# Sparse attention: masks and positions added by VectorE together with the row maximum

## The chip, the cores and the metric

The program runs on one core of one Trainium2 chip. A core has five engines with queues of their own: TensorE (PE; its weight loads are shown apart as PEld), VectorE (DVE), ScalarE (ACT), GpSimd (POOL) and SyncE (SP, which here only issues transfers). The metric is the time of one execution on the device in microseconds (us); lower is better. The kernel before was timed in three runs, and one more execution was profiled.

## The reference, cut to what matters

The model is a decoder trunk of two layers over 512 tokens with width 1024. Layer 1 has, between two feed-forward halves, an attention with three branches over 16 heads of 64, in two groups of keys and values. The change lies in two of the branches, `selected` and `sliding`. With 512 tokens the selection takes all blocks and the window holds all earlier tokens, so both are plain causal softmax attention with positions by slope:

```python
s_s = jnp.einsum('bqghd,bgqnld->bghqnl', qblk, k_sel) - slopes[...] * dist_s
s_s = jnp.where(dist_s >= 0, s_s, NEG)                 # NEG = -1e30
p_s = jax.nn.softmax(s_s.reshape(sh[:4] + (-1,)), axis=-1).reshape(sh)
...
return gblk[..., 0:1] * o_c + gblk[..., 1:2] * o_s + gblk[..., 2:3] * o_w
```

A score is thus q·k, less the head's slope times the distance of query and key, and masked where the key is later than the query. Then `o @ w_out` projects the heads' outputs.

## The kernel before, in words

**Precision.** Products are made of fp32r operands (one pass of TensorE). A value is split into a high part, which fp32r holds exactly, and a low part (the rest). A product then is high x high + high x low + low x high, three matmuls that add up in one PSUM bank (`mm3`, L343 to L345). ScalarE makes the high parts, VectorE or GpSimd the low ones.

**Stages.** `stages` runs `f0, m0, f1, f2, m1, f3, fin`. The change is in `m1` (`mixer1`). Its first part projects keys and values for the two branches (`keys`, `values`), the hidden layer of the compressed branch (`hidden`), and the first queries. Its second part is a loop over steps `t`, written out by hand, whose order of calls is the order of each engine's queue. Its third part is the rest of the output projection.

**Units and steps.** A unit is one pair of heads `m` (8 of them), one head of the two (`hh`) and one branch (`br`): 32 units, three steps each, 96 steps. `m` takes 12 steps. In step t = 3u + x of unit u:

- `scores(u, x)` on TensorE makes the scores of query blocks `JX[x]`: x = 0 blocks 0 and 1 (128 and 256 keys, done with 256 columns each), x = 1 block 2 (384 keys), x = 2 block 3 (512 keys), into one PSUM bank `S` (3 buffers).
- one step later `rowmax` on VectorE takes the negated row maximum, and `exps` on ScalarE writes the exponentials to `P` in SBUF and sums them.
- after the unit's last exponentials `weigh` divides by the sum and applies the branch's gate (VectorE two small instructions, GpSimd four on `P`).
- six steps later `transposes` (TensorE, into one of two PSUM buffers `T`), then `his` (ScalarE) and `lows` (VectorE), which split the transposed weights into `PTh` and `PTl`, and eight steps later `pv` (TensorE) multiplies them with the values into `O`.

Between these the loop puts the query projection of the next m (`qproj`, 24 matmuls of 512 columns, spread over groups of steps by `QP`), its evacuation and split (`qevac` by `QEV`), and the compressed branch of this m (`cmp_step`). From step 77 on no query projection is left; there the table `FILL` puts the split of finished heads' outputs (`osplit`) and the first pieces of the output projection (`oproj`: for output tile d and input tile k, three matmuls of 512 columns).

**The score product before.** `qA` (128 rows) holds q's high part in one half of the partitions and its low part in the other; `kA` holds the keys' high part twice. So one matmul of 128 contraction rows gives high x high + low x high. The second matmul has 68 rows: 64 of q's high part (copied into `qB` by ScalarE or GpSimd) against the keys' low part (`kB`), and four rows that carry the positions (minus slope times query position, in two parts, against ones; the slope in two parts against the key position). Between the two a bf16 matmul adds the mask: the identity (`identb`) times a tile of zeros and -1e30 (`negb`), on the diagonal block. The four rows come by DMA from GpSimd's queue (L1212, L1232).

**What is touched.** `scores`, `rowmax`, `exps` (L1469 to L1505), `qload` and `qevac` (L1224 to L1265), `keys` (L1342), the tiles at the head of `mixer1`, `cmp_step` (a sign), `QEV`, `FILL`, and the constants that `layout` prepares on the host.

Of the kernel before, what the change touches and what calls it, by code (L numbers as in the profile page):

```python
# [20 lines left out]
PLAIN = 2  # L21
DORD = (0, 4, 1, 5, 2, 6, 3, 7)
# [75 lines left out]
def _build(ctx, tc, nc, a, stages):  # L98
# [1096 lines left out]
    def mixer1(nm, nxt):  # L1195
        with ExitStack() as c:
# [3 lines left out]
            identb = sb.tile([128, 128], BF, name="identb")  # L1200
            V.tensor_copy(identb, ident)
            negb = sb.tile([128, 128], BF, name="negb")
# [5 lines left out]
            for br in range(2):  # L1208
                for g in range(2):
                    kA[br, g] = sb.tile([128, T], F32R, name=f"kA{br}{g}")  # L1210
                    kB[br, g] = sb.tile([68, T], F32R, name=f"kB{br}{g}")
                    P.dma_start(kB[br, g][64:68, :], a["keyrows"])  # L1212
                    VS[br, g], V3[br, g] = VSa[:, 2 * br + g], V3a[:, 2 * br + g]
# [11 lines left out]
            def qload(m):  # L1225
                t = aq.tile([128, 4, 2, 32], F32, name="cb", bufs=2)
                nc.sync.dma_start(t, a["cbias"][m])
                bias[m] = t
                qb = []
                for hh in range(2):  # L1230
                    b_ = aq.tile([128, T], F32R, name="qB", bufs=4)
                    P.dma_start(b_[64:68, :], a["qrows"][2 * m + hh])  # L1232
                    qb.append(b_)
                qst[m] = [None, None, qb]
# [10 lines left out]
            def qevac(m, step):  # L1245


                if step == 0:
                    qf = aq.tile([128, T], F32, name="qf", bufs=2)
                    V.scalar_tensor_tensor(qf, qp.pop(m)[0], 0.125, nm.rstd, op0=OP.mult, op1=OP.mult)  # L1250
                    qst[m][0], qst[m][1] = qf, []
                    return
                hh, step = divmod(step - 1, 3)
                r, r2 = slice(hh * 64, hh * 64 + 64), slice(64 - hh * 64, 128 - hh * 64)
                if step == 0:
                    qst[m][1].append(aq.tile([128, T], F32R, name="qA", bufs=3))
                    S.activation(qst[m][1][hh][r, :], qst[m][0][r, :], AF.Copy)
                    return
                t = qst[m][1][hh]
                if step == 1:  # L1260
                    V.tensor_sub(t[r2, :], qst[m][0][r, :], f32(t[r, :]))
                elif hh:
                    P.tensor_copy(qst[m][2][hh][0:64, :], f32(t[r, :]))
                else:
                    S.activation(qst[m][2][hh][0:64, :], f32(t[r, :]), AF.Copy)  # L1265
# [26 lines left out]
            with ExitStack() as c2:  # L1292
                s2 = c2.enter_context(pool("m1t", 1, reuse_waits="tile"))
                ps = c2.enter_context(pool("m1p", 2, space=PSUM, reuse_waits="tile"))
                neg = s2.tile([128, 128], F32, name="neg")
                nc.sync.dma_start(neg, a["neg"])
# [40 lines left out]
                V.tensor_copy(negb, neg)  # L1337
# [4 lines left out]
                def keys(br, key):  # L1342
                    p = pj()
                    proj(p, W.next(key), nm)
                    W.pump(3)
                    kf = s2.tile([128, T], F32, name="kf", bufs=2)
                    V.tensor_mul(kf, p, rstd)
                    k2 = s2.tile([64, T], F32, name="k2", bufs=2)
                    V.tensor_mul(k2, p[64:128, :], rstd[64:128, :])
                    for g in range(2):  # L1350
                        src = kf[0:64, :] if g == 0 else k2
                        S.activation(kA[br, g][0:64, :], src, AF.Copy)
                        S.activation(kA[br, g][64:128, :], src, AF.Copy)
                        V.tensor_sub(kB[br, g][0:64, :], src, f32(kA[br, g][0:64, :]))
# [43 lines left out]
                for part in range(3):  # L1398
# [10 lines left out]
                    if part == 0:  # L1409
                        hidden(1, "v", 2)  # L1410
                        for e in range(4, 7):
                            qevac(0, e)
# [56 lines left out]
            def scores(u, x):  # L1469
                m, hh, br = u  # L1470
                g = m // 4
                qa, qb = qst[m][1][hh], qst[m][2][hh]
                bk = ps.tile([128, T], F32, name="S", bufs=3)
                def half(w, keys, start, stop):
                    for j in JX[x]:
# [3 lines left out]
                                  start=start and j != 1, stop=stop, skip_group_check=True)  # L1479
                        Sb[u, j] = bk[:, c0:c0 + (j + 1) * 128]  # L1480

                half(qa, kA[br, g], True, False)

                if x == 0:
                    d_ = bk.rearrange("p (a b) -> p a b", b=128)[:, 0:4:3, :]
                    TE.matmul(d_, identb, negb[:, None, :].to_broadcast([128, 2, 128]), start=False, stop=False,
                              skip_group_check=True)
                else:
                    j = JX[x][0]
                    TE.matmul(bk[:, j * 128:(j + 1) * 128], identb, negb, start=False, stop=False,  # L1490
                              skip_group_check=True)
                half(qb[0:68, :], kB[br, g], False, True)

            def rowmax(u, x):
                if x == 0:
                    St[u] = at_.tile([128, 64], F32, name="st", bufs=3)[:, 0:16]
                    Pt[u] = at_.tile([128, 1280], F32, name="P", bufs=3)
                for j in JX[x]:
                    V.tensor_reduce(St[u][:, j:j + 1], Sb[u, j], axis=AX.X, op=OP.max, negate=True)

            def exps(u, x):
                st = St[u]
                for j in JX[x]:
                    S.activation(Pt[u][:, OFF[j]:OFF[j] + 128 * (j + 1)], Sb.pop((u, j)), AF.Exp,
                                 bias=st[:, j:j + 1], accum_out=st[:, 4 + j:5 + j])  # L1505
# [59 lines left out]
            def cmp_step(m, step):  # L1565
                if step == 0:
                    p = ps.tile([128, T], F32, name="S", bufs=3)
                    for j in range(4):
# [5 lines left out]
                    V.tensor_add(e, p[:, 0:256].rearrange("p (a b) -> p a b", b=32),  # L1574
                                 bias[m].rearrange("p a h b -> p (a h) b"))
# [42 lines left out]
            QEV = ({8: 0, 9: 1, 10: 2, 12: 3, 14: 4, 16: 6, 19: 5}, {11: 0, 12: 1, 13: 2, 14: 3, 16: 4, 17: 6, 18: 5})  # L1618
# [24 lines left out]
            for m, t in enumerate((78, 79, 81, 83, 86, 90, 97)):  # L1643
                where = (xp, ("xh", 8), ("xl", 8)) if m < 4 else (aq, ("qA", 3), ("qB", 4))
# [153 lines left out]
def layout(i):  # L1798
# [65 lines left out]
    neg = np.where(p[None, :] > p[:, None], f(-1e30), f(0))  # L1864
    slopes = np.array([2.0 ** (-8.0 * (k + 1) / 16) for k in range(16)], dtype=f).reshape(8, 2).T.reshape(16)

    def split(v):
        b = v.astype(f).view(np.uint32)
        hi = (b & np.uint32(0xFFFFF000)).view(f)
        return hi, v.astype(f) - hi  # L1870

    qrows = np.zeros((16, 4, T), f)
    for n in range(16):
        hi, lo = split(-slopes[n] * t.astype(f))
        sh, sl = split(np.full(T, slopes[n], f))
        qrows[n] = np.stack([hi, lo, sh, sl])
    keyrows = np.stack([np.ones(T), np.ones(T), t, t]).astype(f)
    cend = np.arange(31) * 16 + 31
    cb = np.full((8, 128, 4, 2, 32), -1e30, f)
    for m in range(8):  # L1880
# [7 lines left out]
        "poolw": A("a_pool_w")[0].transpose(1, 0, 2).reshape(128, -1), "neg": neg,  # L1888
        "qrows": qrows, "keyrows": keyrows, "cbias": cb,
# [20 lines left out]
```

## Time and profile before

| what | value |
|---|---|
| median of 3 runs | 1874.49 us (1874.49 to 1875.04) |
| profiled execution, its own time | 1873.18 us |
| its span, first to last instruction | 1871.4 us |
| TensorE, matmuls | 1848.3 us, 99% |
| TensorE, weight loads | 1644.1 us, 88% |
| VectorE | 1473.0 us, 79% |
| ScalarE | 968.3 us, 52% |
| GpSimd | 635.7 us, 34% |
| steps 0 to 95 | 1271.9 to 1461.9 us of the span |

A busy time is the union of an engine's instructions, so an engine at 99% has hardly a gap, though a gap-free TensorE may still be slower than it could be: matmuls overlap in its pipeline, and the printed duration of one is longer than the distance to the next start. In the printed forms, `68*128 68x512` is a matmul whose weights have 68 contraction rows and 128 columns, and whose moving operand has 68 rows and 512 columns. fp32r and fp32 both print as f32 there. L1478 is the line of both score products, told apart by `kA` and `kB`.

### The profile page before, as it was taken

How to read it: one execution, taken by the hardware profiler on the slowest of the kernel's cores; microseconds unless marked ns; L12 is line 12 of the kernel's file. 1: busy time of each engine (PE TensorE's matmuls, PEld its weight loads, DVE VectorE, ACT ScalarE, POOL GpSimd, SP SyncE). 2: the span in 40 equal slices, each digit the busy share in tenths (PEclk: the TensorE clock that was granted, in tenths of full speed). 3: DMA queues.
4: the chain of work that ended last, by engine and by line, in shares of the span. 5: the costliest groups of instructions: out<-in, count | busy, mean ns of one | idle time of the engine just before them, and what ended most of it. 6: DMA issues, size and time to landing. Idle time of an engine off the chain costs nothing. (4 is left out here: it accounts for less than half of the span.)

```text
span 1871.4 us, 30811 instructions
## 1 busy us (share of the span) xinstructions
PE 1848.3 (99%) x11564; PEld 1644.1 (88%) x11564; DVE 1473.0 (79%) x2414; ACT 968.3 (52%) x1971; POOL 635.7 (34%) x555
## 2 busy tenths in 40 slices
PE   8999999999999999999999999999999999999998
PEld 6999999778789999998899999878887789999997
DVE  8888887667688888877898887757888679888873
ACT  6445444443455444445454444437888555444443
POOL 2333332203123333312333333114556324333321
PEclk9999999999999999999999999999999999999999
DMA  5232322222233322213223232232100132233221
GB/s 197 80 106 98 109 98 93 85 88 68 79 128 109 102 102 102 102 63 107 102 102 115 100 107 89 88 126 70 30 30 27 57 130 85 102 102 102 102 96 63
DMA packets 62007, 175.12 MB, mean 94 GB/s; under 512 B 7520, under 2 KB 9744, under 8 KB 61856
## 3 DMA queue, kind: packets, MB, share of 16 engines
q1 hardware_dynamic: 60544, 171.68, 27.1%
q8 instruction: 91, 1.49, 0.3%
q10 hardware_dynamic: 576, 1.05, 0.2%
q0 software_dynamic: 736, 0.41, 0.1%
q14 instruction: 60, 0.49, 0.1%
HBM read 171.01 MB, written 2.10 MB: 93 GB/s over the span
## 5 line engine op out<-in xcount | busy, mean ns | idle before, releaser
L542 DVE TENSOR_TENSOR wl<-wr,wh 128x512 fp32r<-128x512 f32 (+1 forms) x312 | 282.1, 926 | 6.0 <-ACT wh L539 2.4
L539 ACT ACTIVATE wh<-wr 128x512 fp32r<-128x512 f32 (+1 forms) x312 | 179.5, 603 | 190.0 <-PE pd L344 172.1
L343 PE MATMUL pd<-ahi,wh 128*128 128x512 f32 x680 | 266.3, 392 | 0.0
L344 PE MATMUL pd<-alo,wh 128*128 128x512 f32 x680 | 266.2, 391 | 0.0
L345 PE MATMUL pd<-ahi,wl 128*128 128x512 f32 x680 | 264.5, 389 | 0.0
L678 DVE TENSOR_TENSOR sl<-T,sh 128x512 fp32r<-128x512 f32 x288 | 242.8, 852 | 22.7 <-ACT sh L677 19.6
L677 ACT ACTIVATE sh<-T 128x512 fp32r<-128x512 f32 x288 | 180.5, 627 | 58.0 <-PE z L714 54.3
L658 POOL TENSOR_TENSOR T<-wg,wr 128x512 f32<-128x512 f32 x36 | 49.8, 1383 | 335.3 <-DMA wg<-in_wts_dram 254.5
L714 PE MATMUL xy<-xh,wl 128*128 128x256 f32 x576 | 163.0, 283 | 0.0
L712 PE MATMUL z<-xs,sh 128*128 128x256 f32 x576 | 163.0, 283 | 0.0
L713 PE MATMUL z<-xs,sh 128*128 128x256 f32 x576 | 163.0, 283 | 0.0
L714 PE MATMUL xy<-xh,sl 128*128 128x256 f32 x576 | 163.0, 283 | 0.0
L713 PE MATMUL xy<-xl,sh 128*128 128x256 f32 x576 | 163.0, 283 | 0.0
L714 PE MATMUL z<-xs,sl 128*128 128x256 f32 x576 | 163.0, 283 | 0.0
L712 PE MATMUL xy<-xh,sh 128*128 128x256 f32 x576 | 163.0, 283 | 0.0
L713 PE MATMUL xy<-xl,wh 128*128 128x256 f32 x576 | 163.0, 283 | 0.0
L712 PE MATMUL xy<-xh,wh 128*128 128x256 f32 x576 | 162.6, 282 | 0.0
L770 DVE SCALAR_TENSOR_TENSOR h<-pd,h 128x512 f32<-128x512 f32 (+1 forms) x157 | 107.1, 683 | 59.9 <-PE pd L345 59.5
L345 PEld LDWEIGHTS pd<-ahi,wl 128*128 128x128 f32 x680 | 127.7, 188 | 27.6
L343 PEld LDWEIGHTS pd<-ahi,wh 128*128 128x128 f32 x680 | 128.2, 189 | 23.1
L344 PEld LDWEIGHTS pd<-alo,wh 128*128 128x128 f32 x680 | 128.2, 189 | 21.4
L658 POOL TENSOR_TENSOR T<-wg 128x512 f32<-128x512 f32 x72 | 108.3, 1504 | 50.6 <-DVE sl L678 50.6
(429 smaller groups left out, 5208.1 us busy)
## 6 DMA issues: line engine op xcount, KB each, us to landing
wr<-in_wts_dram SPq DMA_DIRECT2D x119, 512.0 KB, 3.5
wg<-in_wts_dram SPq DMA_DIRECT2D x72, 512.0 KB, 3.5
wr<-in_wts_dram SPq DMA_DIRECT2D x128, 256.0 KB, 3.7
wf<-in_wts_dram SPq DMA_DIRECT2D x36, 512.0 KB, 4.1
wr<-in_wts_dram SPq DMA_DIRECT2D x32, 384.0 KB, 3.6
h<-in_xt_dram SPq DMA_DIRECT2D x8, 256.0 KB, 4.6
cb<-in_cbias_dram SPq DMA_DIRECT2D x8, 128.0 KB, 3.5
out_dram<-ot ACTq DMA_DIRECT2D x4, 256.0 KB, 2.9
```

Of the source, the lines that this page charges most:

```text
L343: TE.matmul(out, wh, xh, start=first, stop=False)
L344: TE.matmul(out, wh, xl, start=False, stop=False)
L345: TE.matmul(out, wl, xh, start=False, stop=last)
L539: S.activation(w.t[0][:, c], b.t[:, c], AF.Copy)
L542: V.tensor_sub(w.t[1][:, c], b.t[:, c], f32(w.t[0][:, c]))
L658: return lambda: P.tensor_tensor(o.t, x(), y(), op=op)
L677: s = act(T, lambda: S.activation(w.t[0], src(), AF.Copy), (dep,), (w, b))
L678: return w, dve(T, lambda: V.tensor_sub(w.t[1], src(), f32(w.t[0])), (s,), (w, b), True)
L712: TE.matmul(out, wh, xh[:, q], start=start, stop=False, skip_group_check=True)
L713: TE.matmul(out, wh, xl[:, q], start=False, stop=False, skip_group_check=True)
L714: TE.matmul(out, wl, xh[:, q], start=False, stop=k == 3, skip_group_check=True)
L770: return lambda: V.scalar_tensor_tensor(h[d][:, c], b.t[:, c], 0.5, h[d][:, c], op0=OP.mult, op1=OP.add)
```

## The change

The positions and the mask leave TensorE. A host constant `dist` (128 x 512) holds the distance of query and key, 1e30 where the key is later; GpSimd loads it once. For each head GpSimd multiplies it by the slope (`far`, two buffers), three steps before the head's first row maximum. `qevac` gives q the opposite sign, so the bank holds -q·k; VectorE's `tensor_tensor_reduce` then adds the slice of `far`, writes the result to `P` and takes its minimum, and ScalarE's exponential works in place on `P` with scale -1. The second score product has 64 contraction rows: the half of `qA` that holds q's high part, against `kB`, which now holds the keys' low part in both halves. `qB`, its copies, the four rows and the mask products are gone. `QEV` has two entries less for each m. In `FILL` the splits of the outputs move from steps 78-97 to 84-97, and the first tile's pieces from 80, 82, 84, 86, 89, 92, 98 to 88, 90, 90, 94, 94, 96, 98; the second tile's stay.

```diff
+            dist = sb.tile([128, T], F32, name="dist")
+            nc.gpsimd.dma_start(dist, a["dist"])
...
-                    kB[br, g] = sb.tile([68, T], F32R, name=f"kB{br}{g}")
-                    P.dma_start(kB[br, g][64:68, :], a["keyrows"])
+                    kB[br, g] = sb.tile([128, T], F32R, name=f"kB{br}{g}")
...
-                qb = []
-                for hh in range(2):
-                    b_ = aq.tile([128, T], F32R, name="qB", bufs=4)
-                    P.dma_start(b_[64:68, :], a["qrows"][2 * m + hh])
-                    qb.append(b_)
-                qst[m] = [None, None, qb]
+                qst[m] = [None, None]
...
-                    V.scalar_tensor_tensor(qf, qp.pop(m)[0], 0.125, nm.rstd, op0=OP.mult, op1=OP.mult)
+                    V.scalar_tensor_tensor(qf, qp.pop(m)[0], -0.125, nm.rstd, op0=OP.mult, op1=OP.mult)
...
-                if step == 1:
-                    V.tensor_sub(t[r2, :], qst[m][0][r, :], f32(t[r, :]))
-                elif hh:
-                    P.tensor_copy(qst[m][2][hh][0:64, :], f32(t[r, :]))
-                else:
-                    S.activation(qst[m][2][hh][0:64, :], f32(t[r, :]), AF.Copy)
+                V.tensor_sub(t[r2, :], qst[m][0][r, :], f32(t[r, :]))
...
-                        V.tensor_sub(kB[br, g][0:64, :], src, f32(kA[br, g][0:64, :]))
+                        for r in (0, 64):
+                            V.tensor_sub(kB[br, g][r:r + 64, :], src, f32(kA[br, g][0:64, :]))
...
-                qa, qb = qst[m][1][hh], qst[m][2][hh]
+                qa, r = qst[m][1][hh], slice(hh * 64, hh * 64 + 64)
                 bk = ps.tile([128, T], F32, name="S", bufs=3)
-                def half(w, keys, start, stop):
+                for w, keys in ((qa, kA[br, g]), (qa[r], kB[br, g][r])):
                     for j in JX[x]:
                         c0 = 256 if j == 1 else 0
                         n = max(256, 128 * (j + 1))
                         TE.matmul(bk[:, c0:c0 + n], w[:, j * 128:(j + 1) * 128], keys[:, 0:n],
-                                  start=start and j != 1, stop=stop, skip_group_check=True)
+                                  start=w is qa and j != 1, stop=w is not qa, skip_group_check=True)
                         Sb[u, j] = bk[:, c0:c0 + (j + 1) * 128]
 
-                half(qa, kA[br, g], True, False)
-
-                if x == 0:
-                    d_ = bk.rearrange("p (a b) -> p a b", b=128)[:, 0:4:3, :]
-                    TE.matmul(d_, identb, negb[:, None, :].to_broadcast([128, 2, 128]), start=False, stop=False,
-                              skip_group_check=True)
-                else:
-                    j = JX[x][0]
-                    TE.matmul(bk[:, j * 128:(j + 1) * 128], identb, negb, start=False, stop=False,
-                              skip_group_check=True)
-                half(qb[0:68, :], kB[br, g], False, True)
+            far = {}
+
+            def distances(n):
+
+                far[n] = at_.tile([128, T], F32, name="far", bufs=2)
+                P.tensor_scalar(far[n], dist, SLOPES[n], 1.0, op0=OP.mult, op1=OP.mult)
...
                 for j in JX[x]:
-                    V.tensor_reduce(St[u][:, j:j + 1], Sb[u, j], axis=AX.X, op=OP.max, negate=True)
+                    n = 128 * (j + 1)
+                    V.tensor_tensor_reduce(Pt[u][:, OFF[j]:OFF[j] + n], Sb.pop((u, j)), far[2 * u[0] + u[1]][:, T - n:T],
+                                           1.0, 3e38, OP.add, OP.min, St[u][:, j:j + 1])
...
-                    S.activation(Pt[u][:, OFF[j]:OFF[j] + 128 * (j + 1)], Sb.pop((u, j)), AF.Exp,
-                                 bias=st[:, j:j + 1], accum_out=st[:, 4 + j:5 + j])
+                    p = Pt[u][:, OFF[j]:OFF[j] + 128 * (j + 1)]
+                    S.activation(p, p, AF.Exp, bias=st[:, j:j + 1], scale=-1.0, accum_out=st[:, 4 + j:5 + j])
...
-            for m, t in enumerate((78, 79, 81, 83, 86, 90, 97)):
-                where = (xp, ("xh", 8), ("xl", 8)) if m < 4 else (aq, ("qA", 3), ("qB", 4))
+            for m, t in enumerate((84, 84, 87, 89, 90, 92, 97)):
+                where = (xp, ("xh", 8), ("xl", 8)) if m < 4 else (aq, ("qA", 3), ("qB", 1) if m == 6 else ("qf", 2))
...
-            for n, t in enumerate((80, 82, 84, 86, 89, 92, 98, 103, 104, 104, 104, 106)):
+            for n, t in enumerate((88, 90, 90, 94, 94, 96, 98, 103, 104, 104, 104, 106)):
...
                     scores(*at_t(t))
+                if t >= -2 and (t + 2) % 6 == 0 and (t + 2) // 6 < 16:
+                    distances((t + 2) // 6)
```

## Rows read from the trace of the kernel before

**Rows 1.** The page's table of engines: busy us (share) xinstructions.
```profile
PE 1848.3 (99%) x11564; PEld 1644.1 (88%) x11564; DVE 1473.0 (79%) x2414; ACT 968.3 (52%) x1971; POOL 635.7 (34%) x555
```

**Rows 2.** Windows: stretch and length, each engine's busy us, granted clock, DMA.
```profile
1272.00:1425.50 153.50, 152.48 (x988) 128.11 (x987) 127.09 (x314) 125.02 (x372) 85.93 (x137) 1.00 0.10 32
1425.50:1446.20 20.70, 18.53 (x121) 14.92 (x120) 15.76 (x38) 17.37 (x51) 14.59 (x21) 1.00 0.09 27
1446.20:1462.00 15.80, 14.65 (x97) 11.69 (x97) 14.05 (x36) 12.85 (x41) 10.26 (x16) 1.00 0.01 2
1343.02:1366.60 23.58, 23.58 (x158) 19.98 (x155) 19.93 (x49) 19.42 (x58) 13.87 (x22) 1.00 0.09 30
1232.00:1272.00 40.00, 40.00 (x213) 30.91 (x211) 21.91 (x41) 13.26 (x26) 2.54 (x4) 1.00 0.47 166
```

**Rows 3.** Timeline of TensorE, a step with 512 keys: start, duration, line, form.
```profile
1340.45 0.40 PE L1478 MATMUL S<-kA,qA 128*128 128x512 f32 x1
1340.70 0.23 PE L1490 MATMUL S<-negb,identb 128*128 128x128 bf16 x1
1340.74 0.48 PE L1478 MATMUL S<-kB,qB 68*128 68x512 f32 x1
1341.05 0.40 PE L1243 MATMUL X<-xh,wh 128*128 128x512 f32 x1
1341.29 0.40 PE L1243 MATMUL X<-xl,wh 128*128 128x512 f32 x1
```

**Rows 4.** Timeline of TensorE around L915, 48 rows; its third left out.
```profile
373.86 0.39 PE L345 MATMUL pj<-xh,wl 128*128 128x512 f32 x1
374.17 0.69 PE L915 MATMUL at<-grT,gw 48*128 48x512 f32 x1
374.71 0.59 PE L915 MATMUL at<-grT,gw 48*128 48x512 f32 x1
...
375.56 0.59 PE L915 MATMUL at<-grT,gw 48*128 48x512 f32 x1
376.08 0.50 PE L343 MATMUL pj<-xh,wh 128*128 128x512 f32 x1
376.42 0.40 PE L344 MATMUL pj<-xl,wh 128*128 128x512 f32 x1
```

**Rows 5.** Timeline of TensorE around L1429, 62 rows.
```profile
1275.28 0.40 PE L1243 MATMUL X<-xh,wl 128*128 128x512 f32 x1
1275.60 0.46 PE L1429 MATMUL T<-ident,gu 62*128 62x62 f32 x4
1275.99 0.49 PE L1478 MATMUL S<-kA,qA 128*128 128x512 f32 x1
1276.32 0.23 PE L1490 MATMUL S<-negb,identb 128*128 128x128 bf16 x1
```

**Rows 6.** Timeline of TensorE, fp32r with 48 and 16 columns of weights.
```profile
357.91 0.40 PE L882 MATMUL po<-xh,wh 128*48 128x512 f32 x1
358.14 0.40 PE L884 MATMUL po<-xl,wh 128*16 128x512 f32 x1
358.38 0.39 PE L882 MATMUL po<-xh,wh 128*48 128x512 f32 x1
```

**Rows 7.** Waits of 1425 to 1470, then groups of 1272 to 1472: busy, mean ns.
```profile
PEld T L1525 <- DVE PTl L1545: 4.8, 7, 1.1
...
L1499 DVE TENSOR_REDUCE st<-S 128x1 f32<-128x512 f32 x32 | 21.8, 681 | 0.0
...
L1545 DVE TENSOR_TENSOR PTl<-T,PTh 128x512 fp32r<-128x512 f32 x32 | 21.9, 684 | 3.1 <-ACT PTh L1536 3.1
...
L1499 DVE TENSOR_REDUCE st<-S 128x1 f32<-128x128 f32 (+3 forms) x128 | 59.0, 483 | 0.2
...
L1504 ACT ACTIVATION_READ_ACCUMULATOR P<-S,st 128x1 f32 x128 | 25.5, 199 | 0.0
...
L1514 POOL TENSOR_SCALAR P<-P,st 128x512 f32<-128x512 f32 x32 | 27.6, 864 | 0.0
```

More of the change, by code (lines that the diff above doesn't have):

```diff
@@ L21 @@
 PLAIN = 2
+SLOPES = [2.0 ** (-0.5 * (i % 8 * 2 + i // 8 + 1)) for i in range(16)]
 DORD = (0, 4, 1, 5, 2, 6, 3, 7)
@@ L1199, in mixer1 @@
             gts = sb.tile([128, 4, 16, 3], F32, name="gts")
-            identb = sb.tile([128, 128], BF, name="identb")
-            V.tensor_copy(identb, ident)
-            negb = sb.tile([128, 128], BF, name="negb")
+            dist = sb.tile([128, T], F32, name="dist")
+            nc.gpsimd.dma_start(dist, a["dist"])
             VSa = sb.tile([128, 4, 4, 192], F32R, name="VS")
@@ L1249, in qevac @@
                     qf = aq.tile([128, T], F32, name="qf", bufs=2)
-                    V.scalar_tensor_tensor(qf, qp.pop(m)[0], 0.125, nm.rstd, op0=OP.mult, op1=OP.mult)
+                    V.scalar_tensor_tensor(qf, qp.pop(m)[0], -0.125, nm.rstd, op0=OP.mult, op1=OP.mult)
                     qst[m][0], qst[m][1] = qf, []
                     return
-                hh, step = divmod(step - 1, 3)
+                hh, step = divmod(step - 1, 2)
                 r, r2 = slice(hh * 64, hh * 64 + 64), slice(64 - hh * 64, 128 - hh * 64)
@@ L1294, in mixer1 @@
                 ps = c2.enter_context(pool("m1p", 2, space=PSUM, reuse_waits="tile"))
-                neg = s2.tile([128, 128], F32, name="neg")
-                nc.sync.dma_start(neg, a["neg"])
                 R, Z = {}, {}
@@ L1336, in mixer1 @@
                 windows("k")
-                V.tensor_copy(negb, neg)
                 W.pump()
@@ L1410, in mixer1 @@
                         hidden(1, "v", 2)
-                        for e in range(4, 7):
+                        for e in range(4, 5):
                             qevac(0, e)
@@ L1573, in cmp_step @@
                     cm[m] = (e, st)
-                    V.tensor_add(e, p[:, 0:256].rearrange("p (a b) -> p a b", b=32),
-                                 bias[m].rearrange("p a h b -> p (a h) b"))
+                    V.tensor_sub(e, bias[m].rearrange("p a h b -> p (a h) b"),
+                                 p[:, 0:256].rearrange("p (a b) -> p a b", b=32))
                 elif step == 1:
@@ L1617, in mixer1 @@
             at_t = lambda t: (U[t // 3], t % 3) if 0 <= t < 3 * NU else None
-            QEV = ({8: 0, 9: 1, 10: 2, 12: 3, 14: 4, 16: 6, 19: 5}, {11: 0, 12: 1, 13: 2, 14: 3, 16: 4, 17: 6, 18: 5})
+            QEV = ({8: 0, 9: 1, 10: 2, 14: 3, 19: 4}, {11: 0, 12: 1, 13: 2, 16: 3, 18: 4})
             QP = {}
@@ L1863, in layout @@
     gmask = ((p[:, None] // 64 == p[None, :] // 64) & (p[:, None] <= p[None, :])).astype(f)
[L1864 to L1877, printed above, removed]
+    far = (p[:, None] + 384 - np.arange(T)[None, :]).astype(f)
+    far = np.where(far < 0, f(1e30), far)
+    slopes = np.array(SLOPES, dtype=f)
     cend = np.arange(31) * 16 + 31
@@ L1887, in layout @@
         "ident": np.eye(128, dtype=f), "gmask": gmask, "gw2": np.concatenate([A("a_gate_w2")[0], np.zeros((16, 256), f), A("a_gate_w2")[0]]),
-        "poolw": A("a_pool_w")[0].transpose(1, 0, 2).reshape(128, -1), "neg": neg,
-        "qrows": qrows, "keyrows": keyrows, "cbias": cb,
+        "poolw": A("a_pool_w")[0].transpose(1, 0, 2).reshape(128, -1), "dist": far,
+        "cbias": cb,
     }
```

## The prediction

> **What bounds the kernel now.** I read the page first. Its table of engines says TensorE is busy 99% of the span [rows 1], so any TensorE time that goes or comes in a stretch without idle time moves the end. Then the windows of the attention stage [rows 2]: from 1272.0 to 1425.5 us (steps 0 to 77) TensorE is busy 152.48 of 153.50 us, while VectorE has 127.09, ScalarE 125.02 and GpSimd 85.93. The granted clock is 1.00 throughout, the 2.4 GHz level. From 1425.5 to 1462.0 (steps 78 to 95, after the last query projection) TensorE idles 2.17 + 1.15 us; the waits there name the wait of the transposes for VectorE's `PTl` [rows 7]. One m takes 12 steps; in one of them (1343.02 to 1366.60) TensorE works 23.58 of 23.58 us, VectorE 19.93. So the price of a step's score products on TensorE decides, and VectorE matters only once its 19.93 us outgrow TensorE's period.
>
> Last I read TensorE's timeline by starts. Matmuls overlap, so what a matmul costs is not its printed duration (0.40 us) but the distance to the next start, its slot: 0.24 us for a 512-column product [rows 3].
>
> **Part 1: the mask product goes.** In rows 3, one step with 512 keys: `kA` starts at 1340.45, the mask at .70, `kB` at .74, the next projection at 1341.05. Two products and the mask take 0.60 us; two slots of 0.24 would take 0.48, or 0.46 at 0.23. The mask has a slot of only 0.04; the rest is that `kB` starts with its weights not loaded ahead (0.31 instead of 0.23). I take 0.13 us per step, and 96 steps (32 units of 3) make 12.5 us. That is the most this part can give.
>
> **Part 2: the `kB` product shrinks from 68 contraction rows to 64.** The rows cost no time by themselves: a slot goes by columns. But at 64 the product falls into a group for which the trace has rows. L915 (48 rows by 128 columns of weights, in plain fp32, hence its longer slot) stands between 128-row products [rows 4]. The product ahead of it (373.86) takes 0.31 instead of 0.23; L915's first takes 0.54, where its inner ones take 0.43 (374.71 to 375.56 is two slots); its last takes 0.52; the 128-row product behind it 0.34. The excess is 0.08 + 0.11 + 0.09 + 0.10 = 0.38 us for one excursion into the narrow form and back. A second group, L1429 with 62 rows [rows 5], shows the two outer ends: 0.32 before it, and 0.33 for the `kA` behind it, which takes 0.25 in rows 3: 0.17 from these two alone. At both ends the stream stops until what is in flight is through, and the next weights load in the open. At 68 rows nothing of that stands behind `kB`: the projection after it takes 0.24.
>
> What speaks against: L882 and L884 are fp32r as `kB` is, and narrow in the other direction (48 and 16 columns of weights). They take 0.23 and 0.24 [rows 6], no excess at all. No row of before shows an fp32r product with 64 or fewer contraction rows. So its cost lies between 0 (rows 6) and 0.38 (rows 4) per step. I take 0.38, the nearest in what is narrowed: the contraction rows.
>
> The Trainium skill (TensorEngine Tiling (Array Packing), Tiling Modes, Key Properties) states that changing the tiling mode, not just the tile, drains the TensorE. By that rule the change pays at both ends of every step, as in rows 4; by rows 6 the rule doesn't hold for every narrow form, so this trace bears it out for rows and not for fp32r columns. The sum by the rule is the one below; without it the first rival.
>
> Net per step: 0.38 - 0.13 = +0.25 us where a projection product follows the scores, which is in 66 of the 96 steps (8 + 8 + 5 times 10 groups in `QP`). In the other 30 a transpose follows; how late it would be after a narrow product no row shows (between 0 and the 0.10 above); I take 0.05, so +0.20. Sum: 66 x 0.25 + 30 x 0.20 = 16.5 + 6.0 = **+22.5 us**.
>
> **Part 3: the output projection's first pieces move from steps 80-92 to 88-96.** A piece is three products, 0.70 us. Four leave steps 78-87, three more come into steps 88-95. Steps 78-87 (20.70 us now): TensorE 18.53 - 2.8 + 10 x 0.20 = 17.7; VectorE 15.76 plus up to 2.6 (part 4), in a chain with ScalarE, so I take 19.0: -1.7. Steps 88-95 (15.80 now): 14.65 + 2.1 + 8 x 0.20 = 18.35: +2.55. The last piece goes to step 96 or later: +0.4. Together +1.25, where part 2 counted 18 x 0.20 = 3.6 for these steps; so **-2.35**: TensorE's idle time covers that much.
>
> **Part 4: VectorE, ScalarE, GpSimd.** The row maximum was a reduce over PSUM, 681 ns at 512; adding two operands of that size from PSUM and SBUF takes 684 [rows 7]. `tensor_tensor_reduce` does both; no row shows it. Lower bound: the reduce's price, +0. Nearest upper: a separate read of the accumulator as ScalarE's, +199 ns. Per m that is 16 x 0 to 0.199 = 0 to 3.2 us on 19.93, so at most 23.1 in a TensorE period that part 2 stretches to 23.58 + 10 x 0.25 + 2 x 0.20 = 26.5: hidden. I take +0.1 us each, for nothing. If that cover goes (rival 1) it costs.
> The Trainium skill (VectorE: DVE Perf Modes, Two Vector instructions with no wait between them) says that an op which also writes out its accumulator is two instructions. By that the upper half of the bounds is the likelier; the sum stays the same while TensorE's period is the longer.
>
> The new instruction waits for `far` on GpSimd. Behind it on VectorE stand `PTl` and the transposes that wait for that. `far` is issued three steps (some 6 us) ahead; GpSimd is busy 13.87 of 23.58 us, and its 16 scalings at 864 ns [rows 7] replace 16 DMA issues and 8 casts: nothing. Writing `P` must wait until the transposes of three units back have read it; they stand ahead of the same step's scores in TensorE's own queue: nothing. ScalarE's exponentials read SBUF instead of PSUM and one cast in each m goes: off the path. The scores' bank comes free one hop earlier; nobody waits for it now. The four extra subtractions of `kB` lie in 1232 to 1272, where VectorE works 21.91 of 40 us under a TensorE without idle time [rows 2]. On GpSimd's queue one load of `dist` replaces 4 of key rows and the 16 of query rows, and SP loses the load of `neg`: nothing waits for these.
>
> **Sum.** +22.5 - 2.35 = +20.2 us on the profiled execution's own 1873.18 (its span of 1871.4 and 1.8 around it): 1893.3. The median of the runs shown, 1874.49, lies 1.3 above that execution, so I forecast **1895 us**.
>
> **Rivals.**
> *1. The narrow fp32r product costs nothing (rows 6), and the change is not slower.* Then the masks' 12.5 us go: 1862 at best. VectorE decides how much of it stays: its period becomes 19.93 + 0 to 3.2 against TensorE's 23.58 - 12 x 0.13 = 22.0. From 0.13 us more per call it is the bound. In the middle, with its waits for ScalarE, 1.1 us per m is kept, 9 us over the stage: 1866, between 1862 and 1873. For it: fp32r columns. Against it: every group in the trace with 64 or fewer rows that I looked at stands late at both ends.
> *2. VectorE becomes the bound.* If `tensor_tensor_reduce` passes its operands twice, each call costs about another reduce, on average 483 ns [rows 7], 7.7 us per m: 27.7 against TensorE's 26.5. It decides from 0.41 us per call. (27.7 - 23.6) x 8 = 33 us: about 1907.
> *3. Half the excess.* Only the two outer ends of rows 5 come, 0.17 us: (0.17 - 0.13) x 96 = 4 us, less what the tail covers: 1877.
>
> **How the numbers follow.** The forecast has 0.70 of the chance, with a range of its own of 1888 to 1903: down if an excursion costs 0.33, up if transposes are as late as projections and VectorE's longer chain stalls the tail. Rival 1 has 0.19, rival 2 0.05, rival 3 0.06. A range of 1865 to 1905 leaves out the lower part of rival 1, rival 2 and the edge of the forecast, together under 0.2. About 0.2% is what a measurement of this kernel tells from no change, 3.7 us. Rival 1 gives faster 0.14 and same 0.05; rival 3 gives same 0.03 and slower 0.03; the rest is slower: 0.14, 0.08, 0.78.
>
> **What would show it.** Right: TensorE's timeline has no `identb` rows; `kA` at 512 takes about 0.32 to the next start, `kB` (64*128) 0.42, the projection after it 0.34; a period of 12 steps takes 26 to 27 us at 100% TensorE; VectorE's share falls below 85%. Wrong: `kA` and `kB` 0.23 apart with nothing late, and a period near 22 us; or TensorE idle in that period with VectorE full, which is rival 2 or the dear end of rival 1. For part 4, the duration of the new instruction at 512 near 0.69 us and whether a second row stands behind it.

## The result, and the profile after

The changed kernel takes **1890.99 us** (median of 4 runs, 1890.46 to 1891.54), the kernel before 1874.49. The ratio is 1.0089, with a 95% interval from 1.0077 to 1.0101: 0.9% slower. The profiled execution took 1890.81 us, its span 1889.04, against 1871.40 before: 17.64 us more.

The page's table of engines for the changed kernel, busy us, share and instructions, beside [rows 1]:

```profile
PE 1868.8 (99%) x11468; PEld 1644.4 (87%) x11468; DVE 1484.2 (79%) x2544; ACT 970.5 (51%) x1963; POOL 632.3 (33%) x544
```

TensorE has 96 instructions fewer, one mask product per step, and works 20.5 us longer. VectorE has 130 more (most are a second row that each new row minimum brings) and works 11.2 us longer, with its share unchanged.

Windows of the changed kernel with the columns of [rows 2]: steps 0 to 77, steps 78 to 87, steps 88 to 95 (cut 2.1 us after the last score product's start, as there), one m, and the end of the program from the first product `z<-xs,sh` of the last feed-forward stage:

```profile
1272.20:1445.53 173.33, 172.04 (x911) 127.56 (x910) 130.64 (x418) 128.07 (x369) 85.43 (x134) 1.00 0.09 28
1445.53:1464.02 18.49, 17.05 (x98) 12.62 (x98) 15.45 (x51) 15.76 (x45) 10.37 (x17) 1.00 0.09 30
1464.02:1481.52 17.50, 17.50 (x99) 13.08 (x98) 15.14 (x49) 15.28 (x45) 15.40 (x21) 1.00 0.00 1
1379.04:1405.62 26.58, 26.58 (x146) 19.86 (x143) 20.34 (x65) 19.72 (x57) 13.48 (x21) 1.00 0.08 26
1577.43:1889.04 311.61, 304.63 (x2066) 282.74 (x2064) 240.69 (x368) 149.75 (x280) 104.65 (x71) 0.99 0.28 95
```

A period of 12 steps grew from 23.58 to 26.58 us, with TensorE busy throughout in both; VectorE has 20.34 in it, where it had 19.93. The clock is 1.00, the 2.4 GHz level, in all rows of the attention stage, so it is no part of the loss. By stages, from the two traces: the first score product stands 0.39 us later; steps 0 to 77 take 19.62 us more (153.66 to 173.28), steps 78 to 95 up to the last score product 0.49 less, from there to the feed-forward stage's first product 0.67 less, the rest 1.20 less, nearly all of it in the last row above (312.76 before, 311.61 now).

TensorE's timeline in the changed kernel, first a step with 512 keys with a projection product behind the scores, then one with transposes (start, duration, line, form), beside [rows 3]:

```profile
1383.79 0.40 PE L1464 MATMUL S<-kA,qA 128*128 128x512 f32 x1
1384.12 0.49 PE L1464 MATMUL S<-kB,qA 64*128 64x512 f32 x1
1384.54 0.50 PE L1237 MATMUL X<-xh,wh 128*128 128x512 f32 x1
1384.88 0.39 PE L1237 MATMUL X<-xl,wh 128*128 128x512 f32 x1
...
1390.00 0.40 PE L1464 MATMUL S<-kA,qA 128*128 128x512 f32 x1
1390.33 0.50 PE L1464 MATMUL S<-kB,qA 64*128 64x512 f32 x1
1390.76 0.44 PE L1509 MATMUL T<-ident,P 128*128 128x128 f32 x2
1390.95 0.48 PE L1541 MATMUL O<-PTh,VS 128*128 128x512 f32 x1
```

Read by starts: `kA` 0.33 to the next, `kB` 0.42, the projection 0.34. Three products take 1.09 us, where [rows 3] have 0.84 for the same three and the mask. The two longer durations, 0.49 and 0.50, stand at the narrow product and at the one behind it.

Waits of PEld (TensorE's weight loads) from 1272 to 1492 us: in all, times, longest. "issue" means that nothing which the profile shows was waited for:

```profile
PEld S L1464 <- issue: 16.1, 64, 0.4
PEld X L1237 <- issue: 9.5, 45, 0.2
```

The loss has no releaser: these waits name no engine, buffer or transfer. The weight loads of the narrow product and of the projection behind it stand still for 25.6 us in all.

VectorE's new instruction at 512, and the second row behind each of the 128 (groups of 1272 to 1492: busy, mean ns, idle), beside [rows 7]:

```profile
L1482 DVE CUSTOM_DVE_ANT_0 P<-S,far 128x512 f32<-128x512 f32 x32 | 21.9, 683 | 0.2 <-PE S L1464 0.2
...
L1482 DVE DVE_READ_ACCUMULATOR2_ANT st<- 128x1 f32 x128 | 10.6, 83 | 0.0
```

### The profile page after: what moved, and what is told of

Its sections match the earlier page's. It is cut to its first block, busy times and chain, and to the rows that moved or that the text cites. A ratio compares the mean times of both kernels' runs of the same rounds, so it can differ in the third digit from the quotient of the medians.

```text
span 1889.0 us, 30634 instructions
## 1 busy us (share of the span) xinstructions
PE 1868.8 (99%) x11468; PEld 1644.4 (87%) x11468; DVE 1484.2 (79%) x2544; ACT 970.5 (51%) x1963; POOL 632.3 (33%) x544
## 4 chain that ended last, share of the span: by engine, by line
PE 93%; DVE 4%; ACT 1%; DMA 1%; issue 1%; POOL 0%; SPq 0%; POOLq 0%; ACTq 0%; DVEq 0%
PE xy L713 9%; PE xy L715 9%; PE xy L714 9%; PE pd L344 8%; PE pd L345 8%; PE pd L346 8%; PE z L714 4%; PE z L713 4%; PE z L715 4%; PE S L1464 3%; PE X L1237 3%; PE pj L344 2%; PE pj L346 2%; PE pj L345 2%; PE T L1509 2%; PE z L344 2%
## 5 line engine op out<-in xcount | busy, mean ns | idle before, releaser
L543 DVE TENSOR_TENSOR wl<-wr,wh 128x512 fp32r<-128x512 f32 (+1 forms) x312 | 276.6, 908 | 6.1 <-ACT wh L540 2.4
L679 DVE TENSOR_TENSOR sl<-T,sh 128x512 fp32r<-128x512 f32 x288 | 251.9, 883 | 21.1 <-ACT sh L678 18.1
L659 POOL TENSOR_TENSOR T<-wg,wf 128x512 f32<-128x512 f32 x36 | 48.5, 1348 | 231.9 <-DMA wg<-in_wts_dram 214.5
```

The costliest lines, as they stand in the source:

```text
L543: V.tensor_sub(w.t[1][:, c], b.t[:, c], f32(w.t[0][:, c]))
L659: return lambda: P.tensor_tensor(o.t, x(), y(), op=op)
L679: return w, dve(T, lambda: V.tensor_sub(w.t[1], src(), f32(w.t[0])), (s,), (w, b), True)
```

## The experiments

Twelve kernels ran, in groups that shared runs of the kernel before. Its median was 1873.9 to 1874.11 in these groups, and 1874.49 beside the changed kernel, so the times can be set side by side to about 0.6 us. "Full form" below means a second score product over all 128 rows of `qA` against `kB`, which adds the product of the two low parts to the scores.

**Is it the 64 rows? The change without them (e1_full).**

```diff
-                qa, r = qst[m][1][hh], slice(hh * 64, hh * 64 + 64)
+                qa = qst[m][1][hh]
...
-                for w, keys in ((qa, kA[br, g]), (qa[r], kB[br, g][r])):
+                for low, keys in enumerate((kA[br, g], kB[br, g])):
```

> The changed kernel, but the second score product takes all 128 rows of qA against kB, which holds the keys' low part in both halves (it adds low x low). Theory (an excursion into 64 contraction rows is late at both ends): kA's slot at 512 falls from 0.32 to 0.23, kB's from 0.43 to 0.23, the next product's from 0.33 to 0.23; 96 steps x 0.39 = 37 us less on TensorE, a period of 12 steps near 22.1 instead of 26.6 us. VectorE then has about 21.3 us in that period, so some of it may be lost: 1856 to 1866 us. Rival (the new VectorE instruction, not the narrow product, made the change slow): the time stays at 1885 to 1891.

Measured: 1868.87 us (1868.38 to 1869.31), ratio to before 0.9973 [0.9962, 0.9984]. Twice the rows in the product make the kernel 22.1 us faster than the changed one, and faster than before. The same step in its trace:

```profile
1345.78 0.40 PE L1464 MATMUL S<-kA,qA 128*128 128x512 f32 x1
1346.01 0.39 PE L1464 MATMUL S<-kB,qA 128*128 128x512 f32 x1
1346.24 0.40 PE L1237 MATMUL X<-xh,wh 128*128 128x512 f32 x1
1346.47 0.40 PE L1237 MATMUL X<-xl,wh 128*128 128x512 f32 x1
```

Three slots of 0.23 us take 0.69 in place of 1.09: 0.40 for one excursion (into the narrow form and back). But the time is 3 us above the top of what was expected, and one period shows why (columns as in the windows above, then the one row of TensorE's timeline with an idle time in it, in brackets with its releaser):

```profile
1341.79:1365.15 23.36, 22.50 (x145) 19.12 (x143) 20.55 (x65) 19.31 (x58) 13.44 (x22) 1.00 0.10 29
```
```profile
1358.20 0.33 PE L1509 MATMUL T<-ident,P 128*128 128x128 f32 x1 [0.86 <-DVE PTl L1529]
```

TensorE now wants 22.50 us, but the period takes 23.36: in the steps of remainder 8 (counted in twelves) the transposes wait 0.86 us for VectorE.

**Does the narrow product alone bring the loss? The kernel before with 64 rows in its low product (e2_narrow).** The positions are left out of its scores.

```diff
-                half(qb[0:68, :], kB[br, g], False, True)
+                half(qb[0:64, :], kB[br, g][0:64, :], False, True)
```

> The kernel before, with only the second score product cut from 68 to 64 rows (the positions are left out of the scores; masks, row maximum and schedule stay). Theory: the narrow product alone brings the loss; its weights came late behind the mask already, so 0.25 to 0.38 us per step, 24 to 36 us, less 2 to 4 that TensorE's idle time in steps 78 to 95 covers: 1895 to 1907 us. Rival (VectorE's instruction or the moved pieces made the loss): 1872 to 1876 us, as before.

Measured: 1900.87 us (1900.46 to 1901.65), ratio 1.0144 [1.013, 1.0158], within what the theory said. Four rows fewer cost 26.8 us. TensorE's timeline:

```profile
1345.88 0.40 PE L1478 MATMUL S<-kA,qA 128*128 128x512 f32 x1
1346.12 0.23 PE L1490 MATMUL S<-negb,identb 128*128 128x128 bf16 x1
1346.28 0.50 PE L1478 MATMUL S<-kB,qB 64*128 64x512 f32 x1
1346.70 0.50 PE L1243 MATMUL X<-xh,wl 128*128 128x512 f32 x1
1347.04 0.39 PE L1243 MATMUL X<-xh,wh 128*128 128x512 f32 x1
```

1.16 us from `kA` to the second projection product, against 0.84 in [rows 3]. The narrow product costs 0.32 here and not 0.40, since `kB` behind a mask is late anyway (0.31 in place of 0.23). In turn the mask costs only 0.07 beside a narrow product (1.16 to 1.09). So each of the two prices depends on the other; what the change pays is their difference, 0.25 (1.09 less 0.84).

**Each visit, or a mode that lingers? The narrow form for the first head of each pair only (e8_half).**

```diff
-                for w, keys in ((qa, kA[br, g]), (qa[r], kB[br, g][r])):
+                for low, w, keys in ((0, qa, kA[br, g]), (1, *((qa, kB[br, g]) if hh else (qa[0:64], kB[br, g][0:64])))):
```

> The changed kernel, with the low product of 64 rows for the first head of each pair and of 128 rows (low times low added) for the second. Theory (each visit to 64 rows costs its own ends, whatever the other steps do): half of the 22.1 us between the changed kernel and e1_full, 1878 to 1882 us. Rivals: the cost comes once for a stretch, as a clock or a mode that stays, 1888 to 1892; or VectorE's stall covers part of it, 1871 to 1876.

Measured: 1877.25 us (1876.82 to 1877.71), ratio 1.0016 [1.0006, 1.0025]. Its period:

```profile
1348.09:1372.50 24.41, 24.41 (x146) 19.50 (x144) 20.38 (x64) 19.40 (x57) 13.49 (x21) 1.00 0.10 28
```

Six excursions fewer in a period take 26.58 - 24.41 = 2.17 us off, 0.36 each, with TensorE fully busy in both: each visit pays its own ends. The time falls 0.8 below the expected 1878: the first 48 excursions give back 13.7 us, the other 48 only 8.4, since behind them VectorE's stall appears.

**Do the moved pieces matter? The change with the old step numbers in `FILL` (e3_fill).**

```diff
-            for m, t in enumerate((84, 84, 87, 89, 90, 92, 97)):
+            for m, t in enumerate((78, 79, 81, 83, 86, 90, 97)):
...
-            for n, t in enumerate((88, 90, 90, 94, 94, 96, 98, 103, 104, 104, 104, 106)):
+            for n, t in enumerate((80, 82, 84, 86, 89, 92, 98, 103, 104, 104, 104, 106)):
```

> The changed kernel with the old times for the output projection's first tile (80, 82, 84, 86, 89, 92, 98) and for the splits (78 to 97). Theory: moving the pieces hardly matters in the slower stage; put back early they fill idle time of steps 81 to 86 (1.4 us of TensorE idle there) and are missing later: 1889 to 1892 us. Rival (the move is worth 2 to 4 us by itself): 1893 to 1895 us.

Measured: 1891.79 us (1890.77 to 1892.8), ratio 1.0093 [1.0078, 1.0109]; the interval overlaps that of the change nearly whole. First to last score product take 207.22 us there and 207.17 in the change. What the tail covers, it covers with either order. With the full form the same move was tried as **e6_full_fill** (the edit above on e1_full):

> e1_full with the old start times of the output projection's first tile. Theory (at steps of 0.23 us a score product VectorE is late, TensorE stands idle for about 5 us in steps 79 to 86 of e1_full, and pieces put there are done for nothing): 1865 to 1868 us. Rival (as in e3_fill, where the times of the pieces moved nothing): 1869.

Measured: 1869.57 us (1868.97 to 1873.13), ratio 0.9977 [0.9968, 0.9985], as the rival said. Step 80 there takes 5.0 us, and TensorE's timeline names two waits in it, the second brought in by the piece itself:

```profile
1428.42 0.44 PE L1509 MATMUL T<-ident,P 128*128 128x128 f32 x2 [1.82 <-DVE PTl L1529]
1430.45 0.50 PE L345 MATMUL X<-xl,wh 128*128 128x512 f32 x1 [0.89 <-POOL xl L1615]
```

**What does the mask product cost by itself? e1_full with it put back, on a tile of zeros (e9_mask).**

```diff
+                    if low and x == 0:
+                        TE.matmul(bk.rearrange("p (a b) -> p a b", b=128)[:, 0:4:3, :], identb,
+                                  negb[:, None, :].to_broadcast([128, 2, 128]), start=False, stop=False,
+                                  skip_group_check=True)
+                    elif low:
+                        jm = JX[x][0]
+                        TE.matmul(bk[:, jm * 128:(jm + 1) * 128], identb, negb, start=False, stop=False,
+                                  skip_group_check=True)
```

> e1_full with the mask product put back between the two score products, on a tile of zeros, beside VectorE's own adding of the masks. Theory (the mask product costs its own 0.13 us on TensorE, as in the kernel before: 96 times, 12.5 us, of which up to 0.8 us in each of 7 periods can fall into the stall): 1876 to 1882 us. Rival (it is hidden by TensorE's queue of weights or wholly by the stall): 1868 to 1871.

Measured: 1870.42 us (1869.65 to 1871.74), ratio 0.9979 [0.997, 0.9988], as the rival said. One step and the period:

```profile
1347.77 0.40 PE L1476 MATMUL S<-kA,qA 128*128 128x512 f32 x1
1348.01 0.23 PE L1471 MATMUL S<-negb,identb 128*128 128x128 bf16 x1
1348.05 0.47 PE L1476 MATMUL S<-kB,qA 128*128 128x512 f32 x1
1348.36 0.39 PE L1241 MATMUL X<-xh,wh 128*128 128x512 f32 x1
```
```profile
1343.54:1367.01 23.47, 23.47 (x158) 19.92 (x155) 20.18 (x65) 19.46 (x57) 13.52 (x21) 1.00 0.10 29
```

On TensorE the mask costs its 0.12 to 0.13 us (0.04 for itself, `kB` 0.31 in place of 0.23). In the kernel's time 96 of them cost 1.55 us: with the mask TensorE fills a period of 23.47, without it 23.36 pass all the same, 0.86 of them in the stall. So taking the mask away is worth almost nothing while the stall is there. What it is worth without the stall was not run by itself: the fastest kernel below has a period of 22.65, but it was not tried with the mask put back.

**Is it the new instruction that makes VectorE late? e1_full with a plain row minimum from the bank and the exponential reading the bank (e4_reduce).** Masks and positions are left out.

```diff
-                    V.tensor_tensor_reduce(Pt[u][:, OFF[j]:OFF[j] + n], Sb.pop((u, j)), far[2 * u[0] + u[1]][:, T - n:T],
-                                           1.0, 3e38, OP.add, OP.min, St[u][:, j:j + 1])
+                    V.tensor_reduce(St[u][:, j:j + 1], Sb[u, j], axis=AX.X, op=OP.min)
...
-                    S.activation(p, p, AF.Exp, bias=st[:, j:j + 1], scale=-1.0, accum_out=st[:, 4 + j:5 + j])
+                    S.activation(p, Sb.pop((u, j)), AF.Exp, bias=st[:, j:j + 1], scale=-1.0, accum_out=st[:, 4 + j:5 + j])
```

> As the version with 128 rows, but VectorE only takes the row minimum (tensor_reduce) and ScalarE reads the bank: mask and positions are left out of the scores. If VectorE bounds the version with 128 rows, this one is faster by up to 16 x 0.083 x 8 = 10 us. If TensorE bounds it, the two are within 2 us: both near 22.1 us per period of 12 steps, with TensorE without idle time.

Measured: 1872.19 us (1870.95 to 1872.71), ratio 0.9988 [0.9979, 0.9998], 3.3 above e1_full. Neither outcome came. Waits of TensorE from 1300 to 1425 us, the first line from e1_full, the others from e4_reduce, the last of its weight loads:

```profile
PE T L1509 <- DVE PTl L1529: 3.5, 5, 0.9
```
```profile
PE S L1464 <- ACT P L1487: 2.5, 9, 0.4
PE T L1507 <- DVE PTl L1527: 1.6, 5, 0.5
...
PEld S L1464 <- ACT P L1487: 4.4, 9, 0.5
```

The bank is now held until ScalarE has read it, which is a new wait of 2.5 us. The wait for `PTl` falls from 3.5 to 1.6 us, but TensorE comes to it later by the new wait (up to 0.4 us two steps ahead of the stall), so this fall alone does not show that VectorE was earlier. How much of the lateness is the new instruction's stays open.

**Where does VectorE's stall come from?** Four runs on e1_full. The first moves pieces of VectorE's work to other steps (**e5_moved**, together with the old `FILL`):

```diff
-            QEV = ({8: 0, 9: 1, 10: 2, 14: 3, 19: 4}, {11: 0, 12: 1, 13: 2, 16: 3, 18: 4})
+            QEV = ({8: 0, 9: 1, 13: 2, 14: 3, 19: 4}, {11: 0, 12: 1, 13: 2, 16: 3, 18: 4})
...
-            CMP = ({5: 0, 6: 1, 8: 2, 11: 3, 12: 4}, {5: 0, 6: 1, 9: 2, 10: 3, 12: 4})
+            CMP = ({5: 0, 7: 1, 9: 2, 11: 3, 12: 4}, {5: 0, 6: 1, 9: 2, 10: 3, 12: 4})
```

> e1_full with the old start times of the output projection's first tile (step 80 on) and with pieces of VectorE's work moved between steps: a piece of the next queries from 10 to 13, compression pieces from 6 to 7 and from 8 to 9. Theory (once the excursion to 64 rows is gone, what is left in a period is a stall of TensorE of 0.83 to 0.86 us at the steps of remainder 8, where the transposes wait for VectorE, which has more to do in the steps just before): the moved pieces take about 0.8 us out of 6 or 7 periods, 1859 to 1864 us. Rival (the stall only moves with the pieces, to the steps 1 and 3 further on): same as e6_full_fill, 1865 to 1868.

Measured: 1881.47 us (1880.46 to 1882.41), ratio 1.0039 [1.0026, 1.0051]. Neither outcome came: the stall moved and grew, to 0.88 us in the steps of remainder 9 and 0.39 in those of remainder 11, with waits of 0.15 to 0.21 in those of remainders 8 and 2, and a period takes 25.03. Why it grew was not followed up.

The second gives one piece of VectorE's work just before the stall to GpSimd (**e7_pool**), and the third does that with the mask product in place (**e10_pool_mask**, the edit on e9_mask):

```diff
-                    V.tensor_sub(e, e, st[:, 0][:, :, None].to_broadcast([128, 8, 32]))
+                    P.tensor_tensor(e, e, st[:, 0][:, :, None].to_broadcast([128, 8, 32]), op=OP.subtract)
```

> e1_full with one piece of VectorE's work in the jam taken over by GpSimd: the subtraction of the row maximum from the compressed scores (L1563, 128x256, 0.88 us in the steps just before the stall). Theory (the stall of 0.83 us at the steps of remainder 8 is VectorE's, which works without a break from 1352 to 1359 us): most of the stall goes, 6 or 7 times 0.6 to 0.8 us, 1863 to 1866 us. Rival (GpSimd is late instead and the weighing of P with it, or the stall only moves, as in e5_moved): 1869 to 1876.

> e9_mask (the mask product on a tile of zeros put back) with the same subtraction on GpSimd. Theory (TensorE sets the pace in e9_mask already, with no stall left in the periods): nothing to gain, 1869.5 to 1871.5 us, so that the mask product then costs 5 to 8 us between e7_pool and this, where it cost 1.55 between e1_full and e9_mask. Rival (something else than VectorE's work limits both): e7_pool and this differ by 1 to 2 us again.

Measured: 1872.07 us (1871.28 to 1873.65), ratio 0.9991 [0.9982, 1.0], and 1872.95 us (1871.73 to 1873.86), 0.9995 [0.9986, 1.0004]. The theory fell in both, and the rivals came nearer: both are slower than e1_full and e9_mask, and they are 0.9 apart, just under the 1 to 2 that was said. The timelines of e7_pool around the stall show the chain, engine by engine (GpSimd, ScalarE, VectorE, TensorE):

```profile
1357.02 1.29 POOL L218 TENSOR_TENSOR wl<-wr,wh 128x512 fp32r<-128x512 f32 x1
1358.27 0.61 POOL L1563 TENSOR_TENSOR ce<-ce,cst 128x256 f32<-128x256 f32 x1
...
1358.91 0.42 ACT L1564 ACTIVATE ce<-ce 128x256 f32<-128x256 f32 x1 [0.53 <-POOL ce L1563]
1359.23 0.58 ACT L1520 ACTIVATE PTh<-T 128x512 fp32r<-128x512 f32 x1
...
1359.85 0.69 DVE L1529 TENSOR_TENSOR PTl<-T,PTh 128x512 fp32r<-128x512 f32 x1 [0.96 <-ACT PTh L1520]
...
1360.59 0.33 PE L1509 MATMUL T<-ident,P 128*128 128x128 f32 x1 [1.14 <-DVE PTl L1529]
```

GpSimd reaches the subtraction only behind a weight tile's remainder. ScalarE's exponential of the compressed scores waits for it, and behind that in ScalarE's queue stands `PTh`, which nothing keeps waiting but its place in line. VectorE, relieved, idles 0.96 us for `PTh`; the waits name VectorE, but in this kernel VectorE is not the cause. So the last two runs issue that exponential one step later, once with VectorE's subtraction (**e11_later**) and once with GpSimd's (**e12_pool_later**):

```diff
                     V.tensor_reduce(st[:, 0], e, axis=AX.X, op=OP.max)
                     P.tensor_tensor(e, e, st[:, 0][:, :, None].to_broadcast([128, 8, 32]), op=OP.subtract)
+                elif step == 5:
+                    e = cm[m][0]
                     S.activation(e, e, AF.Exp)
...
-            CMP = ({5: 0, 6: 1, 8: 2, 11: 3, 12: 4}, {5: 0, 6: 1, 9: 2, 10: 3, 12: 4})
+            CMP = ({5: 0, 6: 1, 7: 5, 8: 2, 11: 3, 12: 4}, {5: 0, 6: 1, 7: 5, 9: 2, 10: 3, 12: 4})
```

> e1_full with the exponential of the compressed scores (L1564) issued one step later, behind the next step's copies and exponentials in ScalarE's queue. Theory (in e1_full's stall ScalarE's queue and VectorE's are late together: ScalarE waits 0.24 us for VectorE's subtraction, but VectorE itself works without a break up to the remainder PTl that TensorE's buffer waits for): no gain from ScalarE alone, 1868 to 1870 us. Rival (ScalarE's place in line is the whole stall): 1863 to 1866.

> The same later exponential with the subtraction on GpSimd (e7_pool). Theory (in e7_pool the exponential held ScalarE for up to 0.8 us, since GpSimd reached the subtraction only behind its 1.29 us remainder of a weight tile; the copy PTh, VectorE's PTl and TensorE's transposes stood behind it in that order): with both taken out, the stall falls from 1.1 us to 0.3 us or less a period, 1864 to 1867 us, faster than e1_full and the fastest so far. Rival (the stall moves again): 1869 to 1873.

Measured: 1868.44 us (1867.63 to 1870.24), ratio 0.997 [0.996, 0.9981], and **1864.36 us** (1863.68 to 1864.68), ratio 0.9946 [0.9934, 0.9959], the fastest of all, both as the theory said. The period of e12_pool_later, and what is left of its stall:

```profile
1340.38:1363.03 22.65, 22.49 (x146) 19.17 (x143) 19.78 (x65) 19.20 (x57) 14.03 (x23) 1.00 0.10 30
```
```profile
1356.07 0.33 PE L1509 MATMUL T<-ident,P 128*128 128x128 f32 x1 [0.16 <-DVE PTl L1529]
```

Of the two remedies each alone gave nothing (GpSimd +3.2 us, the later exponential -0.4); together they took 4.5 off. The trace of e1_full shows why (ScalarE's line, then VectorE's):

```profile
1356.85 0.58 ACT L1520 ACTIVATE PTh<-T 128x512 fp32r<-128x512 f32 x1
...
1357.29 0.09 DVE L1482 DVE_READ_ACCUMULATOR2_ANT st<- 128x1 f32 x1
1357.46 0.69 DVE L1529 TENSOR_TENSOR PTl<-T,PTh 128x512 fp32r<-128x512 f32 x1
```

`PTh` is done at 1357.43 and VectorE's own earlier work at 1357.38. VectorE's work and ScalarE's place in line were two equally late ways to the same `PTl`.

## Why the prediction was right

The forecast was 1895 us with 1888 to 1903 for its likeliest case; 1890.99 came, and by that case's mechanism. Point by point:

- **The bound.** TensorE's slots set the time: the period grew by 3.00 us with TensorE at 100% in both traces. Forecast: 10 x 0.25 + 2 x 0.20 = 2.90.
- **The narrow product (part 2).** No row of before could settle this choice. The chosen end was right: plain fp32's 48 rows [rows 4] stood for fp32r's 64, and the rows with narrow columns [rows 6] did not, as e2_narrow shows. 0.38 was taken for an excursion with a projection behind it; 0.40 was measured at 512 keys (e1_full) and 0.36 on average over all shapes (e8_half). Where transposes follow, the first one's slot is 0.17 (single starts 1390.76 and 1390.93) against the 0.11 that it has in e9_mask: late by 0.06, taken as 0.05. The page TensorEngine Tiling (Array Packing) of the Trainium skill, section Tiling Modes, Key Properties, says that a change of tiling mode drains TensorE; by that rule each step pays twice, and the trace agrees, with products late at both ends and 0.36 to 0.40 us for the two changes.
- **The mask (part 1).** 0.13 per step was right as TensorE's time beside a full product (e9_mask: 0.12). As what its removal brings by itself it was not: 0.07 beside a narrow product, and 1.55 us in all beside a full one with VectorE late. The sum still comes out, since the 0.38 was priced without a mask ahead of it too.
- **Steps 0 to 77.** 22.5 less the tail's 3.6 is 18.9 forecast; 19.6 came.
- **The tail (part 3) was mis-sized.** 3.6 - 2.35 = +1.25 was forecast for steps 78 to 95 and the last piece; -0.49 and -0.67 came, 2.4 us better. Steps 78 to 87 shrank by 2.21 (1.7 forecast), steps 88 to 95 grew by 1.70 (2.55 forecast), and behind the last score product TensorE's idle time fell from 1.42 to 0.54 us, where 0.4 was added. Two things are in this. From step 78 to the feed-forward stage TensorE's idle time, which the step rightly names as the cover, fell by 2.8 us; and its work there grew by 1.6 us only, where 18 x 0.20 = 3.6 was taken. Why a step costs less there stays open. The moves of the pieces, by which the step reckons, do not matter: with the pieces at their old places the time is the same (e3_fill).
- **VectorE (part 4).** 683 ns and a second row of 83 ns, within 0 to 0.199 and near the 0.1 that was taken; hidden, as said, since its 20.34 us in a period lie under TensorE's 26.58. The page VectorE: DVE Perf Modes of the Trainium skill, section Two Vector instructions with no wait between them, says that an op which also writes out its accumulator is two instructions; the trace agrees, with 128 such rows behind 128 calls.
- **Not foreseen:** the end of the program, which the change does not touch, is 1.15 us shorter (312.76 to 311.61). All kernels built on the change have it (311.4 to 311.6 us), e2_narrow, built on the kernel before, does not (312.80). It lies behind TensorE's last product (up to there TensorE takes 0.18 us longer than before). Windows from the start of that product to the end, before and after:

```profile
1862.82:1871.40 8.58, 0.27 (x3) 0.03 (x1) 1.65 (x3) 1.93 (x3) 0.00 (x0) 0.63 0.67 245
```
```profile
1881.79:1889.04 7.25, 0.27 (x3) 0.03 (x1) 1.65 (x3) 1.93 (x3) 0.00 (x0) 0.76 0.79 289
```

  The engines work equally long in both, so the 1.33 us are not their work, and TensorE, whose granted clock falls here in both, has only the 0.27 us of its last product left. The output's last transfers run there, at 245 and 289 GB/s; what makes this end shorter stays open.
- **The total.** The forecast's +20.2 us against the 17.64 measured: 0.4 came before the first score product, 0.7 more than said in steps 0 to 77, 2.4 less in the tail and 1.2 less behind it. The forecast of 1895 also has in it that the median lay 1.3 us above the profiled execution before; after the change it lay 0.2 above.

Of the rivals, the first (no cost for narrow fp32r) fell with e2_narrow, but its reckoning of what VectorE would then keep can be read from e1_full: 1866 was said, 1868.87 came, and 1862 "at best" against 1864.36 in e12_pool_later. The second needed 0.41 us more per call and got 0.083. The third's half price is refuted by e8_half.

## What to carry to other kernels

Before a product is made narrower to save operands, look in the trace for a product of the same narrow kind among wide ones and read starts, not durations: a few rows less can cost more than a whole product, and rows added for nothing can be the cheaper form. Price a removed instruction together with what then becomes late: 0.12 us of TensorE per step was worth 0.016 in the kernel's time while another queue was late. When a wait names an engine, see whether that engine was itself idle just before: a place in line on a third engine may be the cause, and two equally late causes show no gain until both are gone.

## What the runs showed of the hardware

- Between 68 and 64 contraction rows the price of an fp32r product jumps: `kB` takes 0.31 us behind a mask at 68 rows [rows 3] and 0.42 at 64 (e2_narrow), and the product behind it 0.24 and 0.34.
- The same subtraction on VectorE has very different durations (minimum, median, maximum in ns, then first and last start). The first line is from the kernel before, the second from e1_full:

```profile
L1579 DVE TENSOR_TENSOR ce<-ce,cst x8: 424/426/426, 1284.6 to 1452.3; 128x256 f32<-128x256 f32 x8
```
```profile
L1563 DVE TENSOR_TENSOR ce<-ce,cst x8: 424/882/1140, 1284.7 to 1448.5; 128x256 f32<-128x256 f32 x8
```

  The long calls of e1_full lie beside a subtraction on GpSimd. At 1355.60, where it took 882 ns, GpSimd was in a 1.28 us subtraction (`wl`) that began at 1354.92, so the two ran together for 0.60 us. Over the eight calls the duration goes with that overlap: 424 ns at 0.07 us, 645 at 0.36, 857 to 891 at 0.58 to 0.61, 1001 at 0.71, 1140 at 0.85. In the kernel before no call overlaps one by more than 0.1 us. In the period shown these 0.46 us fall just before the stall of 0.86, so a part of VectorE's lateness may be this meeting and not the amount of its work. On GpSimd the subtraction takes 606 to 627 ns (e7_pool). No run moved the two apart and changed nothing else, so that one slows the other is read from these overlaps and not tried.
